# Queries and keys of two attentions as seven block products with their parts in DRAM, gates among the attention's steps, softmax scaling on ScalarE

## The chip, the cores and the metric

The kernel runs on one core of one Trainium2 chip. A core has a matrix engine (TensorE, PE in the profile), a vector engine (VectorE, DVE), a scalar engine (ScalarE, ACT), a general one (GpSimd, POOL) and a sequencer that issues DMAs (SyncE, SP). Each engine works through its own list of instructions in order, and waits there until what the instruction needs is ready. The metric is the device time of one execution in microseconds (us), the median of several runs.

## The reference

Two layers work on 512 rows of 1024 float32 numbers. A layer projects its input x with one wide matrix, runs three mixers on the pieces, gates and sums them, and ends in a feed-forward block (SwiGLU), with a layer norm after each half. Cut to what matters here:

```python
h = jnp.einsum('bsd,de->bse', x, w_in[l])
rq, rk, rv, rg, cq, ck, cv, dq, dk, dv, gates = jnp.split(h, splits, axis=-1)
o_a = _retention(rq, rk, rv, rg, ret_norm_g[l])
o_b = _chunk_attention(cq, ck, cv, ca_rel_bias[l])          # 8 heads of 64
o_c = _diff_attention(dq, dk, dv, lam, lambda_init, ...)    # 4 pairs of heads of 64
g = jax.nn.sigmoid(gates + b_merge[l]).reshape(B, S, N_BRANCHES, D)
merged = g[:, :, 0] * (o_a @ w_a) + g[:, :, 1] * (o_b @ w_b) + g[:, :, 2] * (o_c @ w_c)
x = _layer_norm(ALPHA * x + merged @ w_out[l], ...)
u_gate, u_up = jnp.split(x @ w_ffn_in[l], 2, axis=-1)
x = _layer_norm(ALPHA * x + (silu(u_gate) * u_up) @ w_ffn_out[l], ...)
```

The four projections cq, ck, dq and dk are 512 columns wide each, cv and dv 512, rv and rg 1024, and the gates 3072. In chunk attention a softmax weight is exp(score) divided by its row's sum. In differential attention the queries and keys are turned by rotary tables first, and each head pair combines two softmaxes, p0 - lam p1, before it is multiplied with the values.

## The kernel before

**Numbers.** Every float32 operand of a matrix product is carried as a pair, a high part rounded by a copy on ScalarE (`part_hi`) and a low part, the rest, subtracted on VectorE (`part_lo`). `mm3` (L122 to L125) makes one product of pairs in three matmuls: high by high, high by low, low by high.

**Weights.** `Wt` (L129) is a weight tile of 256 columns and eight blocks of 128 rows. It is loaded into one of four stage buffers `st` and split into `wh` (ScalarE, L155) and `wl` (VectorE, L156), of which there are three each; the split is done in two halves. `run_items` keeps three weight tiles fetched ahead, so an item's split is in the engines' lists some two items before its matmuls.

**Seven products.** `u_two` (L716) computes two 512-wide projections that share the input as block products by seven instead of eight (the form of Winograd): the input and the weights are cut into 2 x 2 blocks, `Quarters.turned` makes sums of input blocks (`s12`, `s43`), `Adds` (L214) makes sums of weight blocks, partly by loads that accumulate on the way (issued by POOL), and `Staged` (L255) casts and subtracts a 2048-wide block (L261, L262). Before the change three such problems run per layer: the two value projections of chunk and differential attention (`w`), and two for retention's values and gates (`p`, `q`). Each of the seven is a list item of its own, called m1, m2, y, x, g, h, v. `product` puts rows of x on the output's partitions; `product_T`, which the feed-forward part uses, puts output columns there, as two 256-wide matmul groups.

**Queries and keys.** Those of chunk and differential attention are projected directly: `u_cqk(p)` (L869) and `u_dqk(h)` (L937) each project 128 columns of queries and 128 of keys for one pair of heads, 48 matmuls of 512 columns, and hand the result to `QK` (L362), whose `set_q` and `set_k` write the high and low parts into the layout that the scores need: a head's 64 rows in one half of the partitions and another part in the other half. `u_dqk` applies the rotary tables first.

**Attention in steps.** Chunk attention's head h has three steps: `s_c1` (scores, `softmax_num` at L392, then the reciprocal and the scaling by it at L899 on VectorE), `s_c2` (`transpose_triangle` at L407: ten transposes on TensorE, parts on the other engines), `s_c3` (product with the values). In differential attention a head pair has `s_d0` twice (scores of its two heads), `s_d1` (the combination on VectorE, L970), `s_d2` (transposes), `s_d3` (product with the values, copy, squares, a power on POOL, output scaling at L1014) and `s_d4` (transposes of the output and its parts `och`, `ocl`).

**Order.** The items of a layer stand in one list (L1094 to L1112). Beside each item stand groups of steps: `between()` is called after each half of an item and runs the next group, so the steps of the attention lie between halves of projections. The projections are the fill: matmuls that TensorE can do while the other engines work on a softmax. `c(i)` and `d(i)` give the two groups for the i-th place of chunk and differential attention. The build then keeps this order on each engine, with small shifts by its own scheduler. Gates (`u_gate`, 48 matmuls of 512 columns, a tanh) are computed ahead of the branch products (`u_branch`); those named in `EARLY` (six of the twelve) are stored to DRAM and read back, since the 61 slots of the pool `gp` don't hold all. After the third branch's four products comes the output projection with `mg`, the merged result's pairs.

## Time and profile before

| | |
|---|---|
| median of 3 runs | 1900.33 us (1900.01 to 1900.47) |
| profiled execution | 1898.38 us |
| its span in the profile | 1896.5 us |
| mean granted TensorE clock | 0.999 |
| instructions | 26422 |

The span goes from the first to the last instruction of the program; the execution's own time has 1.9 us more around it. All durations quoted from here on are from this one execution.

In the views, PE is the matmul part of TensorE and PEld its weight loads, which run beside the matmuls. A row of the groups gives line, engine, operation, output and inputs with their shapes, how many, then busy time and the mean of one, then idle time just before them and what ended it. A row of the windows gives for each engine its busy time and, in brackets, its number of instructions, then the granted clock of TensorE, the share of the DMA engines and GB/s. A row of a timeline gives start and duration in us; in square brackets stands how long the engine had been idle, and whose result ended that.

### The profile page before, as it was taken

Reading aid. Unit: us, or ns where it says so; the run is one execution under the profiler, and the core shown is the slowest. Engines: PE = TensorE matmul, PEld = TensorE weight load, DVE = VectorE, ACT = ScalarE, POOL = GpSimd, SP = SyncE. Lnnn points to the kernel's source line nnn. Section 1 sums busy time; section 2 is a strip of 40 time slices with the busy share of each in tenths; the row PEclk is TensorE's granted clock in tenths of the full one; section 3 lists DMA queues with packets and bytes.
Section 4 is the critical chain, followed back from the end, with each engine's and each line's share of the span. In section 5 each row is a group of like instructions: output and inputs, shape, how many; then the busy total and the mean of one; then the engine's idle time right before and its main releaser. Section 6 shows DMA issues by size and latency. Waiting matters only on the chain. (4 is left out here: it accounts for less than half of the span.)

```text
span 1896.5 us, 26422 instructions
## 1 busy us (share of the span) xinstructions
PE 1873.9 (99%) x10354; PEld 1630.4 (86%) x10354; DVE 1358.4 (72%) x2065; ACT 957.4 (50%) x1547; POOL 105.5 (6%) x117
## 2 busy tenths in 40 slices
PE   9999999999999999999999999999999999999998
PEld 7788888888888999988898888888888889999886
DVE  5877766667766877787587777566776678877866
ACT  4644555567644444444255546455765344444431
POOL 0000000000001000010000010000000010000100
PEclk9999999999999999999999999999999999999999
DMA  8685443332156387885546835433322654869851
GB/s 264 193 255 141 142 142 127 109 117 87 56 169 187 105 231 177 240 209 151 156 167 195 241 110 166 159 112 97 122 71 80 199 129 145 211 157 266 206 149 45
DMA packets 221745, 297.84 MB, mean 157 GB/s; under 512 B 9534, under 2 KB 116148, under 8 KB 221620
## 3 DMA queue, kind: packets, MB, share of 16 engines
q1 hardware_dynamic: 198388, 250.01, 39.9%
q0 software_dynamic: 23232, 46.14, 14.0%
q8 instruction: 81, 1.33, 0.3%
q14 instruction: 44, 0.36, 0.1%
HBM read 273.00 MB, written 23.12 MB: 156 GB/s over the span
## 5 line engine op out<-in xcount | busy, mean ns | idle before, releaser
L123 PE MATMUL pt<-xTh,wh 128*128 128x512 f32 (+1 forms) x1456 | 506.9, 349 | 1.3 <-ACT wh L261 1.3
L124 PE MATMUL pt<-xTl,wh 128*128 128x512 f32 (+1 forms) x1456 | 502.5, 345 | 2.1 <-DVE xTl L113 1.9
L125 PE MATMUL pt<-xTh,wl 128*128 128x512 f32 (+1 forms) x1456 | 502.1, 345 | 0.0
L262 DVE TENSOR_TENSOR wl<-st,wh 128x2048 fp32r<-128x2048 f32 x126 | 288.1, 2289 | 135.0 <-ACT wh L261 134.7
L261 ACT CAST wh<-st 128x2048 fp32r<-128x2048 f32 x126 | 240.0, 1910 | 227.4 <-PE pt L124 129.1
L124 PEld LDWEIGHTS pt<-xTl,wh 128*128 128x128 f32 x1456 | 276.1, 190 | 34.5 <-DVE xTl L113 2.3
L123 PEld LDWEIGHTS pt<-xTh,wh 128*128 128x128 f32 x1456 | 275.7, 190 | 34.8 <-ACT wh L261 1.7
L125 PEld LDWEIGHTS pt<-xTh,wl 128*128 128x128 f32 x1456 | 275.7, 189 | 34.0
L155 ACT CAST wh<-st 128x1024 fp32r<-128x1024 f32 (+1 forms) x204 | 188.1, 948 | 195.6 <-issue 71.1
L156 DVE TENSOR_TENSOR wl<-st,wh 128x1024 fp32r<-128x1024 f32 (+1 forms) x204 | 219.0, 1095 | 90.6 <-ACT wh L155 84.2
L123 PE MATMUL pf<-wh,hqh 128*128 128x512 f32 x224 | 87.5, 391 | 0.5 <-DVE z L1272 0.5
L124 PE MATMUL pf<-wl,hqh 128*128 128x512 f32 x224 | 87.2, 389 | 0.0
L125 PE MATMUL pf<-wh,hql 128*128 128x512 f32 x224 | 87.1, 390 | 0.0
L123 PE MATMUL pt<-s43h,wh 128*128 128x256 f32 x256 | 72.7, 284 | 2.6 <-ACT wh L261 2.6
L352 ACT COPY sw<-pt 32x512 f32<-32x512 f32 (+1 forms) x96 | 55.6, 579 | 34.8 <-PE pt L125 33.6
L123 PE MATMUL pt<-s12h,wh 128*128 128x256 f32 x256 | 72.4, 283 | 0.0
L124 PE MATMUL pt<-s12l,wh 128*128 128x256 f32 x256 | 72.4, 283 | 0.0
L125 PE MATMUL pt<-s12h,wl 128*128 128x256 f32 x256 | 72.4, 283 | 0.0
L124 PE MATMUL pt<-s43l,wh 128*128 128x256 f32 x256 | 72.4, 283 | 0.0
L125 PE MATMUL pt<-s43h,wl 128*128 128x256 f32 x256 | 72.4, 283 | 0.0
L123 PE MATMUL pf<-wh,xTh 128*128 128x512 f32 x144 | 56.3, 391 | 0.0
L125 PE MATMUL pf<-wh,xTl 128*128 128x512 f32 x144 | 56.2, 391 | 0.0
(284 smaller groups left out, 3834.6 us busy)
## 6 DMA issues: line engine op xcount, KB each, us to landing
st<-in_w_in SPq DMA_DIRECT2D x60, 1024.0 KB
st<-in_w_ffn_in SPq DMA_DIRECT2D x40, 1024.0 KB
st<-in_w_ffn_out SPq DMA_DIRECT2D x24, 1024.0 KB
st<-in_w_in SPq DMA_DIRECT2D x32, 512.0 KB
st<-in_w_ffn_in POOLq DMA_DIRECT2D x16, 1024.0 KB, 10.4
st<-in_w_ffn_out POOLq DMA_DIRECT2D x16, 1024.0 KB, 9.8
st<-in_w_in POOLq DMA_DIRECT2D x12, 1024.0 KB, 11.2
th<-th SPq DMA_DIRECT2D x48, 256.0 KB
```

What stands on the lines that cost most here:

```text
L123: nc.tensor.matmul(ps, lh, rh, start=start, stop=False, skip_group_check=more)
L124: nc.tensor.matmul(ps, lh, rl, start=False, stop=False, skip_group_check=more)
L125: nc.tensor.matmul(ps, ll, rh, start=False, stop=stop, skip_group_check=more)
L155: return [nc.scalar.copy(self.hi[:, a:b], self.st[:, a:b]), nc.vector.tensor_sub(self.lo[:, a:b], self.st[:, a:b], f(self.hi[:, a:b]))]
L156: nc.vector.tensor_sub(self.lo[:, a:b], self.st[:, a:b], f(self.hi[:, a:b]))]
L261: nc.scalar.copy(self.hi, st)
L262: nc.vector.tensor_sub(self.lo, st, f(self.hi))
L352: nc.scalar.copy(sw[half * b:half * b + half], ps[half * o:half * o + half])
```

## The change

- **Queries and keys.** `u_cqk` and `u_dqk` go. The chunk attention's two projections become one problem of seven products (`cc`), the differential attention's another (`dd`), both by `u_two` with `product_T`. Each assembled result (128 columns of the output by two times 256 rows) goes through `qk_away`: rotary where it belongs, high and low part on whole 128 x 512 tiles, and a store of each to DRAM. Before a head pair's scores, `qk_back` makes a `QK` and `fetch` reads its parts back in ten DMAs of 64 x 512. The zeros in `kl` that POOL writes stay. The rotary tables are loaded in halves (`rot_tables`), and the mask of differential attention has a step of its own (`mask`).
- **Gates.** The gate items stand among the attention's steps, where the direct projections stood; all but the last of them go through DRAM. Gate (0, 3) stands inside `dd`.
- **Two steps in a place.** c(5) with c(6) share one item, and d(6) with d(7).
- **Last branch.** Three of its four products become one item, `u_branch_by_row(2, 3, 2)`: six results in six PSUM banks, with the row blocks outside, and the last pair's transposes, value product and output transposes (`s_d4(2)`, `s_d2(3)`, `s_d3(3)`, `s_d4(3)`) between the row blocks. `branch_done` is the end of a branch product, unchanged and put into a function.
- **Weights** are split whole instead of in halves.
- **Scaling.** The chunk attention's division by the softmax sum goes from VectorE to ScalarE.

Over the program TensorE's list has 768 matmuls of 512 columns fewer and 1344 of 256 columns more; SP's has 746 DMAs instead of 482.

```diff
-EARLY = [(0, 0), (0, 1), (0, 2), (0, 3), (2, 0), (2, 1)]
+EARLY = [(br, i) for br in range(3) for i in range(4)][:-1]
...
             self.load(0, nk)
-            h = max(nk // 2, 1)
-            for a in range(0, nk, h):
-                self.split(a, min(a + h, nk))
+            self.split(0, nk)
...
-        def set_q(self, src, scale):
...
-        def set_k(self, src):
...
+        def fetch(self, away, c):
+
+            (qh, ql), (kh, kl) = away["q"], away["k"]
+            for j, own, oth in ((0, A, B), (1, B, A)):
+                for to, rows, src in ((self.q[j], own, qh), (self.q[j], oth, ql), (self.k[j], own, kh),
+                                      (self.k[j], oth, kh), (self.kl[j], own, kl)):
+                    nc.sync.dma_start(f(to[rows]), src[own, c])
...
-        def u_two(left, right, left_done, right_done):
+        def u_two(left, right, left_done, right_done, prod=product):
...
-                        use(j, functools.partial(product, xq, name, j, wt))
+                        use(j, functools.partial(prod, xq, name, j, wt))
...
-        def u_cqk(p):
...
+        def qk_away(away, name, scale, rot=None):
+
+
+            away[name] = [dram.tile([P, 2048], F32, name=f"{name}{part}{l}_{'cd'[rot is not None]}") for part in "hl"]
+
+            def done(i, src):
+                half, b = divmod(i, 2)
+                if rot is not None:
+                    src = rotary(src, rot["cd"][half], rot["sd"][half], 32)
+                hi, lo = g(F32R, "qkh"), g(F32R, "qkl")
+                part_hi(hi, src, scale)
+                part_lo(lo, src, hi, scale)
+                for t, to in zip((hi, lo), away[name]):
+                    to = to.rearrange("p (q c) -> p q c", c=512)[:, 2 * b:2 * b + 2, 256 * half:256 * half + 256]
+                    nc.sync.dma_start(to, f(t).rearrange("p (q c) -> p q c", c=256))
+            return done
+
+        def qk_back(qk, away, p):
+            def fn():
+                qk[p] = QK()
+                qk[p].fetch(away, slice(512 * p, 512 * p + 512))
+            return fn
...
-                    nc.vector.tensor_scalar_mul(e, e, r[:, nt:nt + 1])
+                    nc.scalar.activation(e, e, AF.Identity, scale=r[:, nt:nt + 1])
...
-        def u_dqk(h):
...
+        def rot_tables():
...
+        def mask():
...
+        def u_branch_by_row(br, n, m):
...
+            def fn(*wts):
+                act = (oa, ob, oc)[br]
+                jobs = [(wts[i], P * j, bank("pt")) for i in range(n) for j in range(2)]
+                th_ = [gate_of(br, d) for d in range(2 * n)]
+
+                def rows(k0, k1, jobs):
+                    for k in range(k0, k1):
+                        for wt, c0, ps in jobs:
+                            mm3(ps, wt.hi[:, k, c0:c0 + P], wt.lo[:, k, c0:c0 + P], act[k].hi, act[k].lo,
+                                k == 0, k == nk - 1)
+
+                for k in range(nk - 1):
+                    rows(k, k + 1, jobs[:2 * m])
+                    between()
+                rows(0, nk - 1, jobs[2 * m:])
+                between()
+                rows(nk - 1, nk, jobs)
+                for d, (t, job) in enumerate(zip(th_, jobs)):
+                    branch_done(br, d, t, job[2])
+            return [([w[:, 256 * i:256 * i + 256]], nk) for i in range(n)], fn
...
+        caw, daw = {}, {}
         w, p, q = u_two(CV, DV, v_away(cv, 64), v_away(dv, 128, -1.0)), u_rvg(0), u_rvg(1)
+        cc = u_two(CQ, CK, qk_away(caw, "q", CA_DH ** -0.5), qk_away(caw, "k", None), product_T)
+        dd = u_two(DQ, DK, qk_away(daw, "q", DA_DH ** -0.5, tabs), qk_away(daw, "k", None, tabs), product_T)
+        cb, db = functools.partial(qk_back, cqk, caw), functools.partial(qk_back, dqk, daw)
         for (specs, fn), *groups in [
...
-            (u_gate(2, 0), [s_r2(2)], [s_r2(3), s_r3(2)]), (u_cqk(1), [s_r3(3)] + c(0)[0], c(0)[1]),
-            (u_branch(0, 0), c(1)[0] + [v_back(cv)], c(1)[1]), (u_branch(0, 1), *c(2)), (u_cqk(2), *c(3)),
-            (u_branch(0, 2), *c(4)), (u_cqk(3), *c(5)), (u_branch(0, 3), *c(6)), (u_gate(2, 1), *c(7)),
-            (u_dqk(0), *c(8)), (u_gate(1, 0), [v_back(dv)], [s_c3(7)] + d(0)[1]), (u_branch(1, 0), *d(1)), (u_dqk(1),),
-            (u_gate(1, 1), *d(2)), (u_branch(1, 1), *d(3)), (u_dqk(2),),
-            (u_gate(1, 2), *d(4)), (u_branch(1, 2), *d(5)), (u_dqk(3),),
-            (u_gate(1, 3), *d(6)), (u_branch(1, 3), *d(7)), (u_gate(2, 2), [s_d4(2)], [s_d2(3)]),
-            (u_gate(2, 3), [s_d3(3)], [s_d4(3)]),
-            (u_branch(2, 0),), (u_branch(2, 1),), (u_branch(2, 2),), (u_branch(2, 3),),
...
+            (w["m1"],), (w["m2"], [lam]), (w["y"],), (w["x"],), (w["g"], [], [p["a"]]), (w["h"],), (w["v"], [s_dh(0)], [p["c"]]),
+            (p["m1"], [], [s_r1(0)]), (p["m2"], [s_dh(1)]), (p["y"], [], [s_r1(1)]), (p["x"],), (p["g"], [], [cc["a"]]),
+            (p["h"],), (p["v"], [], [cc["c"]]),
+            (cc["m1"], [], [s_r2(0)]), (cc["m2"],), (cc["y"], [s_r2(1)], [s_r3(0)]), (cc["x"], [], [s_r3(1)]),
+            (cc["g"], [], [dd["a"]]), (cc["h"], [rot_tables]), (cc["v"], [], [dd["c"]]),
+            (dd["m1"],), (dd["m2"],), (u_gate(0, 3),), (dd["y"],), (dd["x"],), (dd["g"], [], [q["a"]]), (dd["h"],),
+            (dd["v"], [], [q["c"]]),
+            (u_rqk(rq, RQ, 1),), (q["m1"], [s_dh(2)]), (u_rqk(rk, RK, 1),), (q["m2"], [], [s_r1(2)]), (q["y"], [s_dh(3)]),
+            (q["x"], [], [s_r1(3)]), (q["g"],), (q["h"], [], [cb(0)]), (q["v"],),
+            (u_gate(1, 0), [s_r2(2)], [s_r2(3), s_r3(2)]), (u_gate(1, 1), [s_r3(3)] + c(0)[0], c(0)[1]),
+            (u_branch(0, 0), [cb(1)] + c(1)[0] + [v_back(cv)], c(1)[1]), (u_branch(0, 1), *c(2)),
+            (u_branch(0, 2), [cb(2)] + c(3)[0], c(3)[1]), (u_branch(0, 3), *c(4)),
+            (u_gate(1, 2), [cb(3)] + c(5)[0] + c(5)[1], c(6)[0] + c(6)[1]), (u_gate(1, 3), *c(7)),
+            (u_gate(2, 0), [db(0), mask] + c(8)[0], c(8)[1] + [v_back(dv)]), (u_gate(2, 1), [], [s_c3(7)] + d(0)[1]),
+            (u_branch(1, 0), [db(1)] + d(1)[0], d(1)[1]), (u_branch(1, 1), *d(2)), (u_gate(2, 2), [db(2)] + d(3)[0], d(3)[1]),
+            (u_branch(1, 2), *d(4)), (u_branch(1, 3), [db(3)] + d(5)[0], d(5)[1]),
+            (u_gate(2, 3), d(6)[0] + d(6)[1], d(7)[0] + d(7)[1]),
+            (u_branch_by_row(2, 3, 2), [s_d4(2)], [s_d2(3)], [s_d3(3)], [s_d4(3)]), (u_branch(2, 3),),
```

Of the item list the first half of the removed lines and the unchanged ones are cut. How the lists of the engines move is shown at three places; a row has line, operation, output and inputs by the program's names, the shape, and how many follow each other.

The first place is TensorE's list at the first pair of differential attention in the first layer, at the transposes of the combined softmax `dE`. `xT` is the layer's input, `ob` the output of chunk attention, `wh` and `wl` the weights' parts. Before:

```order
L124 MATMUL pt<-xTl,wh 128x512
L125 MATMUL pt<-xTh,wl 128x512
L417 MATMUL ptr<-ident,dE 128x128 x10
L123 MATMUL pt<-xTh,wh 128x512
L124 MATMUL pt<-xTl,wh 128x512
```

and after:

```order
L124 MATMUL pt<-obl,wh 128x512
L125 MATMUL pt<-obh,wl 128x512
L412 MATMUL ptr<-ident,dE 128x128 x10
L123 MATMUL pt<-obh,wh 128x512
L124 MATMUL pt<-obl,wh 128x512
```

Before, 72 matmuls of 512 columns stand between the second scores of the pair and these transposes, projections and a gate; after, twelve, half of a branch product.

The second place is ScalarE's list at the second pair's second scores. L404 before and L399 after are the exponentials with their sums; L155 and L153 are casts of weights, L1044 a gate's tanh; the numbers tell buffers apart. Before:

```order
L1006 ACTIVATE junk_3907,ss_3905<-do_3906 128x128 x2
L155 CAST wh_3995<-st_3994 128x512 x2
L404 ACTIVATE dE_3961,sums_3964<-dE_3961,mx_3965 128x512
L404 ACTIVATE dE_3962,sums_3964<-dE_3962,mx_3965 128x384
L404 ACTIVATE dE_3963,sums_3964<-dE_3963,mx_3965 128x256
L404 ACTIVATE dE_3962,sums_3964<-dE_3962,mx_3965 128x128
L352 COPY sw_4035<-pt_4010 32x512 x4
```

and after:

```order
L1015 ACTIVATE junk_4690,ss_4688<-do_4689 128x128 x4
L153 CAST wh_4792<-st_4791 128x2048
L1044 ACTIVATE th_4754<-pt_4729,hb_370 128x512
L399 ACTIVATE dE_4758,sums_4761<-dE_4758,mx_4762 128x512
L399 ACTIVATE dE_4759,sums_4761<-dE_4759,mx_4762 128x384
L399 ACTIVATE dE_4760,sums_4761<-dE_4760,mx_4762 128x256
L399 ACTIVATE dE_4759,sums_4761<-dE_4759,mx_4762 128x128
L109 ACTIVATE och_4819<-pdt_4814,colv_368 128x512
```

Before, two quarter-size casts stand ahead of the exponentials; after, a whole cast (into a `wh` that an earlier item holds) and the tanh of the gate that is being computed.

The third place is VectorE's list at the end of the third branch in the first layer. L1065, L1069 and L115 are the gate's product, the sum over branches and the low part of the merged result `mgl`; L156 before and L154 after subtract the weights' low parts. Before:

```order
L156 TENSOR_TENSOR wl<-st,wh 128x512
L1065 SCALAR_TENSOR_TENSOR th<-th,pt 128x512
L1069 TENSOR_TENSOR th<-th 128x512
L115 SCALAR_TENSOR_TENSOR mgl<-th,mgh 128x512
L156 TENSOR_TENSOR wl<-st,wh 128x512 x2
L1065 SCALAR_TENSOR_TENSOR th<-th,pt 128x512
L1069 TENSOR_TENSOR th<-th 128x512
L115 SCALAR_TENSOR_TENSOR mgl<-th,mgh 128x512
L156 TENSOR_TENSOR wl<-st,wh 128x1024 x2
L1065 SCALAR_TENSOR_TENSOR th<-th,pt 128x512 x2
L1069 TENSOR_TENSOR th<-th 128x512 x2
L1065 SCALAR_TENSOR_TENSOR th<-th,pt 128x512
```

and after:

```order
L1065 SCALAR_TENSOR_TENSOR th<-th,pt 128x512 x2
L115 SCALAR_TENSOR_TENSOR mgl<-th,mgh 128x512
L1069 TENSOR_TENSOR th<-th 128x512 x2
L1065 SCALAR_TENSOR_TENSOR th<-th,pt 128x512
L115 SCALAR_TENSOR_TENSOR mgl<-th,mgh 128x512
L1069 TENSOR_TENSOR th<-th 128x512
L115 SCALAR_TENSOR_TENSOR mgl<-th,mgh 128x512
L1065 SCALAR_TENSOR_TENSOR th<-th,pt 128x512
L115 SCALAR_TENSOR_TENSOR mgl<-th,mgh 128x512
L1069 TENSOR_TENSOR th<-th 128x512
L115 SCALAR_TENSOR_TENSOR mgl<-th,mgh 128x512
L154 TENSOR_TENSOR wl<-st,wh 128x1024
```

Before, the low parts of weights alternate with one or two results' operations; after, seventeen full-width operations (thirteen of these rows' and four of the same lines just ahead of them) stand in a row ahead of the 1024-wide `wl`, which belongs to the last branch product.

61 lines of the change are left out of this document (21 added, 40 removed).

## The prediction

> **What bounds the kernel now.** First the page's head, the busy shares and the slices.
>
> ```profile
> span 1896.5 us, 26422 instructions
> PE 1873.9 (99%) x10354; PEld 1630.4 (86%) x10354; DVE 1358.4 (72%) x2065; ACT 957.4 (50%) x1547; POOL 105.5 (6%) x117
> PE   9999999999999999999999999999999999999998
> ```
>
> TensorE is busy in 1873.9 of 1896.5 us, in every slice. So time falls only with its own work, and any wait given to it is added in full. Next, its groups with shapes kept apart, and windows that hold one shape alone.
>
> ```profile
> L123 PE MATMUL pt<-xTh,wh 128*128 128x512 f32 x848 | 334.6, 395 | 0.0
> L123 PE MATMUL pt<-s43h,wh 128*128 128x256 f32 x256 | 72.7, 284 | 2.6 <-ACT wh L261 2.6
> ```
>
> ```profile
> core 0: us, PE busy (x) PEld busy (x) DVE busy (x) ACT busy (x) POOL busy (x), PEclk, DMA share, GB/s
> 29.00:61.70 32.70, 32.70 (x145) 27.09 (x145) 23.17 (x34) 18.08 (x25) 2.96 (x3) 1.00 1.02 296
> 613.00:652.00 39.00, 39.00 (x328) 39.00 (x327) 35.37 (x54) 20.05 (x30) 0.66 (x1) 1.00 0.14 48
> 399.00:476.00 77.00, 77.00 (x388) 65.54 (x387) 56.90 (x124) 52.18 (x118) 5.22 (x8) 1.00 0.28 90
> ```
>
> A matmul's own 395 or 284 ns overlap with the next; its price is the pitch: 32.7/145 = 0.2255 us for 512 columns and 39.0/328 = 0.119 us for 256, more than half, so narrow products give a part back. The third window is differential attention today: TensorE never waits while VectorE is busy 56.9 of 77 us, because full-width projections stand between the attention's steps.
>
> **The change part by part. The matmuls.** Per layer, four 512-wide projections are 384 matmuls of 512 columns. Two problems of seven products are 2 x 7 x 48 = 672 of 256. Both layers: -768 x 0.2255 = -173.2, +1344 x 0.119 = +159.8 us, together **-13.4 us**. Every other matmul stays.
>
> **The waits in differential attention.** Between the first scores and the last output of a layer stand today, as fill, three query/key items and five gates of 48 full-width matmuls each (10.8 us) and four branch-1 items of 24 (5.4); afterwards two gates, the four of branch 1 and the by-row item. The second scores of a head pair are followed by the pair's combination, and its transposes stood 16 us of fill later; now a half branch item or a half gate is there. How long the chain from scores to transposes takes is in the timelines of today's first pair, PE, DVE and ACT in turn.
>
> ```profile
> 406.18 0.39 PE L387 MATMUL psc<-ks,qs 128*128 128x512 f32 x1
> 407.39 0.44 PE L123 MATMUL pt<-xTh,wh 128*128 128x512 f32 x1
> ```
>
> ```profile
> 406.99 1.29 DVE L1069 TENSOR_TENSOR th<-th 128x512 f32<-128x512 f32 x2
> 408.19 0.68 DVE L402 CUSTOM_DVE_ANT_0 dE<-psc,mask 128x512 f32<-128x512 f32 x1
> 411.30 0.18 DVE L964 RECIPROCAL rec<-sums 128x4 f32<-128x4 f32 x1 [0.18 <-ACT dE L404]
> 411.98 1.94 DVE L970 SCALAR_TENSOR_TENSOR dE<-dE,rec 128x128 f32<-128x128 f32 x4
> 438.91 0.16 DVE L1010 SCALAR_TENSOR_TENSOR ss<-ss,sums 128x4 f32<-128x4 f32 x1 [0.76 <-ACT junk L1006]
> 440.26 1.31 DVE L1014 TENSOR_SCALAR do<-do,rsr 128x128 f32<-128x128 f32 x4 [1.19 <-POOL rsr L1011]
> ```
>
> ```profile
> 408.98 0.72 ACT L404 ACTIVATE dE<-dE,mx 128x512 f32<-128x512 f32 x1 [1.33 <-DVE mx L402]
> 411.08 0.19 ACT L404 ACTIVATION_READ_ACCUMULATOR dE<-dE,mx 128x1 f32 x1
> ```
>
> Columns: start, duration, line, operands, idle before. Scores take 1.2 us (406.18 to 407.39). From VectorE's first reduction, 408.19, the exponentials end 3.1 us later (411.27) and the combination 5.7 us later (411.98 + 1.94). A full-width VectorE operation has a pitch of 0.60 us (two from 406.99 to 408.19). Zero below is the start of a pair's second scores; ten transposes need 1.0 us.
>
> *Pair 0.* TensorE reaches the transposes after 1.2 + 12 x 0.2255 = 3.9 us. VectorE's order has a half split and branch operations first (reductions from 0.9) and one more add behind the reciprocal: 0.9 + 5.7 + 0.6 = 7.2; the last four transposes end at 7.7 instead of 4.9: **2.8**.
>
> ```profile
> L261 ACT CAST wh<-st 128x2048 fp32r<-128x2048 f32 x126 | 240.0, 1910 | 227.4 <-PE pt L124 129.1
> L262 DVE TENSOR_TENSOR wl<-st,wh 128x2048 fp32r<-128x2048 f32 x126 | 288.1, 2289 | 135.0 <-ACT wh L261 134.7
> L1035 ACT ACTIVATE th<-pt,hb 128x512 f32<-128x512 f32 x8 | 5.5, 684 | 3.5 <-PE pt L125 3.4
> L156 DVE TENSOR_TENSOR wl<-st,wh 128x1024 fp32r<-128x1024 f32 x26 | 31.3, 1222 | 5.8 <-ACT wh L155 2.9 <-PE ptr L417 2.6
> ```
>
> *Pair 1.* ScalarE's order has the cast of the next gate's weights ahead of the exponentials, and it waits for a buffer that the present gate gives back at zero: 1.91 + 0.68 for the tanh puts them at 2.6, their end at 4.9. Behind it VectorE does the reciprocal's group (0.7), a branch operation, a low part and an add (1.8), the combination (1.94): 9.3, transposes to 9.7 instead of 1.2 + 2.7 + 0.4 + 1.0 = 5.3: **4.4**. *Pair 2* has, by VectorE's order, a half split (1.22), pair 1's output scaling and two branch operations (1.2) among its four reductions. The scaling waits for POOL (ss at 438.91 to do at 440.26: 1.35, then 1.31), so the last reduction ends at 7.4, exponential and reciprocal's group at 8.1, the combination at 10.0 and the transposes at 10.3. TensorE has 1.2 + 5.4 + 0.4 + 1.0 + 0.4 = 8.4 without a wait: **2.0** at least. *Pair 3*: pair 2's output is scaled at 6.0, its transposes are reached at 3.9 (2.0); pair 3's own combination costs 0.3 more; its output runs through copies, squares, POOL and scaling for 5 us beside 18 matmuls (4.1 us), 0.9, and ScalarE's half of that output is waited for by the next matmul, 0.9: **4.1**.
>
> *The end of the by-row item.* Six results end within 3 us and each needs three full-width VectorE operations. The split of the last item's weights (wl, 1.22) stands behind 17 of them: 17 x 0.60 + 1.22 = 11.4 us, 12.0 with the casts it alternates with. TensorE can do 20 matmuls meanwhile (4.5 us): **7.5**. Before, each pair of results has 5.4 us of matmuls beside it.
>
> Per layer 2.8 + 4.4 + 2.0 + 4.1 + 7.5 = 20.8, twice **41.6 us**. Bounds: 0, as in the window 399 to 476, and about 30 per layer if each chain also queues behind ScalarE. I take the chains, since their rows are those of the same instructions.
>
> **The clock.** The end of the program shows what a long rest does.
>
> ```profile
> 1886.00:1890.00 4.00, 1.44 (x7) 0.86 (x5) 3.93 (x7) 0.00 (x0) 0.92 (x1) 1.00 0.31 120
> 1891.50:1896.50 5.00, 0.00 (x0) 0.00 (x0) 1.45 (x3) 0.00 (x0) 0.00 (x0) 0.50 0.29 107
> ```
>
> ```profile
> 83.30 0.39 PE L125 MATMUL pf<-wh,s12l 128*128 128x512 f32 x1
> 86.72 0.50 PE L123 MATMUL pf<-wh,s43h 128*128 128x512 f32 x1 [3.03 <-ACT tu L731]
> 87.06 0.40 PE L124 MATMUL pf<-wl,s43h 128*128 128x512 f32 x1
> ```
>
> The granted clock is 0.50 some 4 us after the last matmul, while after 3.03 idle us it hardly shows (87.06 - 86.72 = 0.34). So the 7.5 us wait should dip, and the others perhaps not. No row shows the return to full rate; between 0 and the 4 us that the fall takes I take 3 us at half rate, 1.5 lost, twice **3.0 us** (bounds 0 and 4 x 2). The Trainium skill's "TensorE: Matmul & The Clock Gate", Part 1, says that an idle window of about 3.4 us halves the clock and that as much busy time restores it. By it the 4.4 us wait dips too, four dips of 1.7 = 6.8, and the sum ends 3.8 us later; both rows agree with its limit, and no run here shows the return.
>
> **Transfers.** Accumulating loads have their own queue.
>
> ```profile
> q1 hardware_dynamic: 198388, 250.01, 39.9%
> q0 software_dynamic: 23232, 46.14, 14.0%
> ```
>
> ```profile
> 62.00:115.00 53.00, 49.97 (x221) 41.07 (x220) 37.25 (x47) 27.50 (x37) 2.56 (x2) 1.00 0.72 221
> 1000.00:1060.00 60.00, 60.00 (x266) 49.66 (x265) 43.20 (x58) 31.92 (x44) 2.56 (x2) 1.00 0.76 227
> ```
>
> 250.01 MB in 39.9% of 1896.5 us is 330 GB/s, 46.14 in 14.0% is 174. A problem loads 5.24 MB plainly and 2.10 accumulating (15.9 + 12.1 us); with 4.19 MB of parts written (12.7) it needs 40.7 us, beside 336 x 0.119 = 40.0 us of matmuls. Value, chunk and differential problems are like this, and the gate that stands in the first one today moves out. Of today's two value problems (0.72 and 0.76 share) one waits 3.03 us and one does not, so I add one such wait, **3.0 us** (bounds 0 and six, 18). A store that waits on SP for its low part holds the weight loads queued behind it, and TensorE needs those two items later.
>
> **Costed at nothing.**
>
> ```profile
> L899 DVE TENSOR_SCALAR cE<-cE,rec 128x512 f32<-128x512 f32 x8 | 3.9, 482 | 0.0
> ```
>
> The softmax scaling, four operations of at most 0.482 per head, leaves VectorE for ScalarE; an item's matmuls stand between it and the transposes (uncovered: 1.9 x 16 heads). Reading a pair back is 1.3 MB, 4 us at 330 GB/s, issued two items ahead (uncovered 4 x 16). Casts of whole 2048-wide weights instead of halves, rotary on assembled rows, extra adds: they lie beside 40 us per problem, in which VectorE has nine full-weight operations (20.6) and fourteen of 0.60 (8.4), 29 us; the differential problem's rotary adds 24 x 0.60 = 14.4 and its gate a split, 46 of 51 us. What doesn't fit would be a wait for weights of up to one cast, 1.91. POOL's clears are unchanged.
>
> **Sum.** -13.4 + 41.6 + 3.0 + 3.0 = +34.2 us: span 1930.7. The profiled execution's 1898.38 becomes 1932.6; the median of the runs, 1900.33, lies 1.95 above it: **1934.5 us**.
>
> **The rivals.** *Faster.* The fill suffices: for it, today's attention windows without any wait, and VectorE's average of 74%. It decides where the five waits of a layer fall below 6.7 us in sum; with none, 1900.3 - 13.4 = 1886.9. Against it: two of them (4.4, 7.5) hang on orders in which one instruction stands behind another. Chance 0.13. *Half the waits.* Pairs 0, 2 and 3 find VectorE free, only 4.4 and 7.5 stay: -13.4 + 23.8 = +10.4, 1910.7; chance 0.13. *Transfers bind.* Six waits of 3.0 instead of one: 1949.5; for it, 40.7 us of transfers in 40.0; against, 296 GB/s at a share of 1.02 in the window 29 to 61.7 with no wait; 0.12. *The clock dips at every wait over 4 us*, the 4.4 too: four dips of 1.7 instead of 3.0, 1938.3; 0.15, since 3.03 us left the rate full and about 4 us halved it, and 4.4 lies at the edge. The Trainium skill's page named above is for it. *That the seven products aren't made*: no, the order shows 1344 matmuls of 256 columns for 768 of 512.
>
> **How the numbers follow.** The forecast has 0.47. The range, 1906 to 1955, takes in half the waits and the transfers with some 5 us for the unknown costs at both ends; outside it are the faster case (0.13), 0.03 below 1906 and 0.04 above. 0.2% (3.8 us) is what a measurement of this kernel can tell from no change. Faster 0.13, same 0.03, slower 0.84.
>
> **What would show it.** Right: TensorE idle of 2 to 8 us at the transposes of dE (released by the combination line), and one of 7 us before the last item's pt matmuls, released by wl; the slices of TensorE below 9 near both attention ends; product groups of 2.9 us per 24. Wrong: no idle there, or one as long before the first product of a problem, released by a DMA.

## The result, and the profile after

The changed kernel takes 2025.46 us (median of 4 runs, 2020.88 to 2026.46), the kernel before 1900.20 in the same comparison: 1.0654 times as long, 95% interval 1.0636 to 1.0673. The direction was forecast; the size was not: 125 us were lost where 34 were expected, and the time lies 70 us above the range. The page's head of the profiled execution (2020.88 us), busy shares, TensorE's slices and its granted clock:

```profile
span 2019.1 us, 28019 instructions
PE 1912.4 (95%) x10930; PEld 1677.0 (83%) x10930; DVE 1366.3 (68%) x1916; ACT 972.6 (48%) x1486; POOL 112.0 (6%) x125
PE   9989989999899999999999899899998899999998
PEclk9989989999899999999999999898998999999999
```

The span is 122.6 us longer. Two lines carry this. TensorE rests 2019.1 - 1912.4 = 106.7 us instead of 22.6, **84.1 more**. And it is busy 38.5 us longer, though its list should have become 13.4 us shorter: its matmuls took **51.9 us more** than at the pitches of before. Five of the clock row's six dents stand in slices where PE has one too. The waits of TensorE, grouped by what released them (us in total, times, longest):

```profile
PE ptr L412 <- DVE dE L979: 18.0, 6, 4.8
PE pf L123 <- ACT tm L726: 16.1, 2, 8.1
PE pt L125 <- DVE wl L154: 13.4, 2, 6.7
PE pco L934 <- DVE cPl L113: 9.0, 4, 3.0
PE pf L123 <- ACT tu L726: 8.4, 4, 4.9
PE pt L123 <- ACT wh L153: 7.4, 3, 3.7
PE pco L934 <- DMA vhl<-v: 6.5, 6, 2.2
PE pf L123 <- DVE rtmp L782: 6.2, 3, 5.3
PE pt L123 <- ACT och L109: 1.6, 2, 0.8
```

By place: differential attention 18.0 + 13.4 + 1.6 = 33.0 us; the block products and the gate behind them 16.1 + 8.4 + 7.4 + 6.2 = 38.1; chunk attention 9.0 + 6.5 = 15.5. Only the first of these places had a large term in the prediction. (A wait is given here as the idle time that the views show; the expectations further down count it from the starts of the matmuls, which makes the same wait 0.1 to 0.2 us longer.)

The slower matmuls are for the most part a matter of the clock. In this windows view the columns are those of before; the first row is a wait of 8 us, the next two what follows, the last two the same behind the by-row item:

```profile
287.80:295.80 8.00, 0.00 (x0) 0.00 (x0) 7.16 (x10) 4.77 (x7) 0.00 (x0) 0.70 0.84 264
295.90:300.90 5.00, 5.00 (x12) 3.66 (x13) 4.00 (x7) 2.84 (x6) 0.00 (x0) 0.50 0.28 94
300.90:305.90 5.00, 5.00 (x27) 4.31 (x26) 3.73 (x7) 2.15 (x4) 0.00 (x0) 0.97 0.00 0
603.60:610.20 6.60, 0.03 (x1) 0.00 (x0) 6.60 (x12) 3.40 (x6) 0.00 (x0) 0.86 0.00 0
610.30:614.70 4.40, 4.39 (x10) 3.47 (x11) 4.40 (x3) 0.00 (x0) 0.00 (x0) 0.50 0.70 235
```

After a wait the granted clock is 0.50 for some 5 us, and 12 matmuls of 512 columns fill 5.0 us (0.417 each instead of 0.2255). TensorE counts as busy in them. The trace's record of the granted clock has 19 such stretches ahead of the program's end, each 3.4, 6.8 or 10.2 us long, 116 us together; the kernel before has none there. TensorE is busy in 89.7 of these 116 us, and half of that, some 45 us, is what the half rate costs (an estimate); the other 7 of the 51.9 us it does not explain.

What VectorE waited for, of DMAs, in the kernel before and then in the changed one:

```profile
DVE th L1065 <- DMA th<-th: 10.4, 8, 2.9
DVE tb L891 <- DMA tb<-nrel: 0.9, 1, 0.9
```

```profile
DVE th L1065 <- DMA th<-th: 25.4, 12, 6.0
DVE tb L901 <- DMA tb<-nrel: 22.4, 11, 5.9
DVE rtmp L782 <- DMA dh<-in_decay: 10.0, 3, 5.1
```

The gates read back, the bias tables and the decay tables are late now. On average the plain queue has room (it went from 39.9% to 45.1%). What holds a table back shows in the timeline of the changed kernel in chunk attention, SyncE's, VectorE's and ScalarE's rows in turn:

```profile
444.58 0.59 SPq L377 DMA_DIRECT2D kl<-kl_c  x1
445.27 0.53 SPq L892 DMA_DIRECT2D tb<-nrel  x1
449.30 0.11 DVE L901 MEMSET tb<- 64x64 f32 x1 [5.94 <-DMA tb<-nrel]
449.34 0.11 DVE L905 RECIPROCAL rec<-sums 128x4 f32<-128x4 f32 x1
449.37 0.65 DVE L113 TENSOR_TENSOR cPl<-ptr,cPh 128x512 fp32r<-128x512 f32 x1
449.48 1.92 ACT L909 ACTIVATE cE<-cE,rec 128x128 f32<-128x128 f32 x4 [4.21 <-DVE rec L905]
451.31 0.56 ACT L107 CAST cPh<-ptr 128x512 fp32r<-128x512 f32 x1
```

Ten reads of a pair's queries and keys are issued from 438.95 to 445.2, one behind the other; the next head's bias table comes after them and is there at 449.3. VectorE stands 5.94 us at the memset of that table. Behind it in its list are this head's reciprocal and a low part (`cPl`) for which TensorE waits; ScalarE stands at the scaling, which needs the reciprocal, and behind the scaling is the cast for TensorE's next wait. The DMA engines are half free in the four us before the table lands, but full at the other waits of chunk attention, those for its values `vhl` (share and GB/s stand at the end):

```profile
445.30:449.30 4.00, 1.80 (x8) 1.14 (x7) 0.00 (x0) 0.00 (x0) 0.00 (x0) 1.00 0.52 145
386.00:390.00 4.00, 1.89 (x9) 1.22 (x8) 1.62 (x3) 2.25 (x5) 0.00 (x0) 0.99 1.07 385
```

### The profile page after: what moved, and what is told of

It is laid out like the page before. It is cut to its first block, busy times and chain, and to the rows that moved or that the text cites. A ratio compares the mean times of both kernels' runs of the same rounds, so it can differ in the third digit from the quotient of the medians.

```text
span 2019.1 us, 28019 instructions
## 1 busy us (share of the span) xinstructions
PE 1912.4 (95%) x10930; PEld 1677.0 (83%) x10930; DVE 1366.3 (68%) x1916; ACT 972.6 (48%) x1486; POOL 112.0 (6%) x125
## 3 DMA queue, kind: packets, MB, share of 16 engines
q1 hardware_dynamic: 213364, 303.51, 45.1%
## 5 line engine op out<-in xcount | busy, mean ns | idle before, releaser
L123 PE MATMUL pt<-xTh,wh 128*128 128x256 f32 (+1 forms) x1392 | 461.2, 332 | 9.3 <-ACT wh L153 7.4
L124 PE MATMUL pt<-xTl,wh 128*128 128x256 f32 (+1 forms) x1392 | 458.4, 330 | 1.9 <-DVE xTl L113 1.6
L125 PE MATMUL pt<-xTh,wl 128*128 128x256 f32 (+1 forms) x1392 | 457.9, 329 | 0.0
L260 DVE TENSOR_TENSOR wl<-st,wh 128x2048 fp32r<-128x2048 f32 x154 | 352.3, 2290 | 132.3 <-ACT wh L259 131.0
L259 ACT CAST wh<-st 128x2048 fp32r<-128x2048 f32 x154 | 293.6, 1909 | 246.7 <-PE pt L124 139.4
L154 DVE TENSOR_TENSOR wl<-st,wh 128x2048 fp32r<-128x2048 f32 (+2 forms) x91 | 171.9, 1892 | 149.4 <-ACT wh L153 118.5
L153 ACT CAST wh<-st 128x2048 fp32r<-128x2048 f32 (+2 forms) x91 | 144.1, 1587 | 233.6 <-PE pt L124 99.3
L123 PEld LDWEIGHTS pt<-s43h,wh 128*128 128x128 f32 x384 | 73.6, 192 | 3.0 <-ACT wh L259 3.0
L123 PEld LDWEIGHTS pt<-s12h,wh 128*128 128x128 f32 x384 | 73.7, 192 | 0.1
L124 PEld LDWEIGHTS pt<-s12l,wh 128*128 128x128 f32 x384 | 73.7, 192 | 0.1
## 6 DMA issues: line engine op xcount, KB each, us to landing
st<-in_w_in POOLq DMA_DIRECT2D x20, 1024.0 KB, 11.6
```

Source lines behind the costliest of these rows:

```text
L123: nc.tensor.matmul(ps, lh, rh, start=start, stop=False, skip_group_check=more)
L124: nc.tensor.matmul(ps, lh, rl, start=False, stop=False, skip_group_check=more)
L125: nc.tensor.matmul(ps, ll, rh, start=False, stop=stop, skip_group_check=more)
L153: return [nc.scalar.copy(self.hi[:, a:b], self.st[:, a:b]), nc.vector.tensor_sub(self.lo[:, a:b], self.st[:, a:b], f(self.hi[:, a:b]))]
L154: nc.vector.tensor_sub(self.lo[:, a:b], self.st[:, a:b], f(self.hi[:, a:b]))]
L259: nc.scalar.copy(self.hi, st)
```

## The experiments

All ratios are to the kernel before on the same chip; "the changed kernel" stands for 1.0654 (1.0636 to 1.0673). A step of 0.001 is 1.9 us, and "us less" is worked out from the ratios. Busy and idle times are those of the one profiled execution of each kernel.

**The reads of queries and keys from another queue.**

```diff
-                    nc.sync.dma_start(f(to[rows]), src[own, c])
+                    nc.gpsimd.dma_start(f(to[rows]), src[own, c])
```

> The 160 reads of queries and keys are issued by GpSimd instead of SyncE; nothing else is changed. Theory (SyncE's queue): each of these small reads takes SyncE 0.55 to 0.6 us to issue, ten are 5.6 us, and the bias tables, the chunk values and the gates that stand behind them in its list land late; VectorE or TensorE wait for those. Then the waits of TensorE at 387 to 394 us (2.3 + 0.8 + 0.9) and at 447 to 453 (3.1 + 2.1) of the first layer go, and their like in the second, 18 us in all, with some 6 us of half-rate matmuls behind them: about 2000 us. Rival (transfers as such): the bytes and packets are the same, so the waits stay, and the time is within 5 us of the changed kernel's 2025. Second rival: GpSimd issues them no faster and behind its accumulating loads, so the reads themselves come late and the wait moves to the scores: within 10 us either way.

2018.89 us, 1.0636 (1.0612 to 1.0660): no difference from the changed kernel that is clear of the noise. The waits in chunk attention went, all but some 2 us a layer, but the first wait of differential attention grew from 4.8 to 11.4 us, and from 4.4 to 10.9 in the second layer. The waits of this kernel's TensorE and VectorE have these rows:

```profile
PE ptr L412 <- DVE dE L979: 29.7, 4, 11.4
DVE th L1065 <- DMA th<-th: 37.0, 15, 6.9
```

And VectorE's timeline, between the two scores of the first pair:

```profile
498.54 0.69 DVE L1065 SCALAR_TENSOR_TENSOR th<-th,pt 128x512 f32<-128x512 f32 x1 [6.95 <-DMA th<-th]
```

VectorE now stands at a gate read back. So the place in SyncE's list was the cause at the bias table of 449 us, where VectorE's wait fell from 5.94 to 1.33. (For bias tables in all it still waits 23.5 us, mostly where TensorE does not wait for it.) GpSimd also issues the reads earlier (the second pair's from 356.7 us instead of 374.5), so at the chunk values, where the DMA engines are full, place and transfers are not told apart. In differential attention the next late load of SyncE's list took the gain away.

**The reads half an item earlier** (`cb` and `db` moved behind the scores of the pair before).

> The changed kernel with each head pair's reads of queries and keys (all but the first pair of each attention) put half an item earlier in the list, behind the scores of the pair before, so that bias tables, chunk values and gate reads no longer stand behind ten of them. Still all on SyncE, the same bytes. Theory (place in SyncE's queue): the waits in chunk attention (9.2 and 8.9 us a layer) fall to 4 or less a layer, and the first wait in differential attention (4.9), of which VectorE's 1.6 us for a gate is a part, to about 3; with the half-rate stretches some 18 us less, a ratio to before of about 1.056. Rival (too many bytes or packets at these places): the waits stay, and the ratio is 1.062 or more.

2048.23 us, 1.0793 (1.0775 to 1.0811): 26 us worse. VectorE's waiting for gates rose to 43.9 us in 13 times; the first wait in differential attention became 8.0 us. The ratio is the rival's, 1.062 or more. That moving the ten reads forward put the gates behind them is a reading of the order in SyncE's list; no further run tells it from the rival's reason, too many bytes at these places.

**Bias tables two heads ahead, the second branch's gates an item earlier.**

> The changed kernel with chunk attention's bias tables loaded two heads ahead instead of one, and the gates of the second branch read back an item earlier; the reads of queries and keys stay where they are. Theory (VectorE stands in its list at a small load that lands late): of the waits in chunk attention those released by parts of transposed weights go (3.1 + 2.1 us a layer), those for chunk values stay (2.3 + 0.8 + 0.9); the first two waits in differential attention (4.9, 3.9) lose the 1.6 and 0.9 us in which VectorE waits for a gate. Some 7 us a layer with 2 us of dips: 15 to 20 us less, a ratio to before of 1.055 to 1.058. Rival (the queue as a whole is behind, so that what is put first makes another load late, as when the reads were put earlier): 1.062 or more.

2023.34 us, 1.0651 (1.0636 to 1.0667): no change. VectorE's waits for bias tables fell only to 17.7 us. The first differential wait was 5.5 us with the gate there in time, for the build had put operations on branch results ahead of the second reductions, as VectorE's timeline of this kernel shows:

```profile
512.28 0.69 DVE L1074 SCALAR_TENSOR_TENSOR th<-th,pt 128x512 f32<-128x512 f32 x1 [0.99 <-PE pt L125]
513.00 0.69 DVE L1078 TENSOR_TENSOR th<-th 128x512 f32<-128x512 f32 x1
513.61 0.68 DVE L397 CUSTOM_DVE_ANT_0 dE<-psc,mask 128x512 f32<-128x512 f32 x1
```

The rival held. Which load is late depended on the order; that some load is late at these places did not, in the orders tried here.

**The decay table two items earlier.**

```diff
-(w["g"], [], [p["a"]]), (w["h"],), (w["v"], [s_dh(0)], [p["c"]]),
+(w["g"], [s_dh(0)], [p["a"]]), (w["h"],), (w["v"], [], [p["c"]]),
```

> The first decay table of retention is loaded two items earlier (beside w's g instead of w's v). Theory: the 5.5 us wait of TensorE at 112 us of the first layer is VectorE's wait of 5.1 us for this load, which is issued behind six stores and lands 11 us later. It goes, with the half-rate stretch behind it (3.0 us): 8 us less; the next wait (3.1 us at 133) stays. Rival: VectorE has too much to do there, and the bank would come free late anyway: less than 3 us.

2014.72 us, 1.0613 (1.0594 to 1.0632), 8 us less. In the timeline of the changed kernel, SyncE's rows and then VectorE's, the table is issued behind six stores and VectorE waits 5.1 us for it:

```profile
99.02 6.17 SPq L847 DMA_DIRECT2D v<-vhl  x6
105.25 0.46 SPq L765 DMA_DIRECT2D dh<-in_decay  x1
116.67 0.69 DVE L782 TENSOR_TENSOR rtmp<-psr,dh 128x512 f32<-128x512 f32 x1 [5.10 <-DMA dh<-in_decay]
```

The 6.2 us of waits released by `rtmp` went, but those released by `tu`, one item later, rose from 8.4 to 12.2, and TensorE's rest as a whole fell by 1.2 us only (from 106.7 to 105.5); its busy time fell by 4.9. The 8 us are the theory's number, then, but only in part its mechanism: the next wait, which was to stay, grew.

**The last split ahead of the results** (the by-row item's six results are finished inside the next item).

```diff
...
                 act = (oa, ob, oc)[br]
+                while late:
+                    branch_done(*late.pop(0))
                 for j in range(2):
...
-                for d, (t, job) in enumerate(zip(th_, jobs)):
-                    branch_done(br, d, t, job[2])
+                late.extend((br, d, t, job[2]) for d, (t, job) in enumerate(zip(th_, jobs)))
```

> The six results of the by-row item are finished inside the last branch item, so that the split of the last item's weights stands ahead of all but two of their seventeen VectorE operations. Theory (as predicted: the low part of the last weights is late because it stands behind them): the wait of 6.9 us before the last branch product falls to 2 or less in each layer, with the half-rate stretch behind it (2.0 us): 10 to 14 us less in all. Rival: the splits of the output projection's weights now come ahead of the results, and the wait moves to the first output products, which need the merged result: less than 4 us.

2003.58 us, 1.0552 (1.0534 to 1.0571), 19 us less, more than the theory's 10 to 14. The 13.4 us of waits released by `wl` are gone, and no new row took their place; the other waits grew by some 4 us in all (TensorE's rest is 97.4 us instead of 106.7), and its busy time fell by 8.1. VectorE's timeline has the split behind two operations instead of seventeen:

```profile
602.70 1.28 DVE L1067 SCALAR_TENSOR_TENSOR th<-th,pt 128x512 f32<-128x512 f32 x2 [0.96 <-PE pt L125]
604.02 1.22 DVE L154 TENSOR_TENSOR wl<-st,wh 128x1024 fp32r<-128x1024 f32 x1
```

**Without rotary in the differential problem** (left out, so its queries and keys are not turned).

> The rotary step of the differential attention's queries and keys is left out (four copies on ScalarE, three operations on VectorE for each of 16 results). Theory (VectorE and ScalarE fall behind in that problem, and the copies and parts of retention's queries stand behind it in their lists): the waits at 287 us (8.2) and 320 us (3.8) of the first layer and their like in the second fall below 3 us in sum per layer, with their half-rate stretches (2.3 + 1.6): about 25 us less. Rival: these waits come from retention's own rotary and decay steps, which stand close together now: at most 5 us less.

1995.96 us, 1.0514 (1.0491 to 1.0536), 27 us less. The 16.1 us released by `tm` are gone, 7.4 became 4.4 at the gate, and the 6.2 released by `rtmp` became 2.8, while those released by `tu` rose from 8.4 to 11.1. The theory held: in the window 287.8 to 295.8 above VectorE is busy 7.16 of 8 us while TensorE rests; the parts and rotary of retention's queries stand in its list behind the end of the differential problem.

**Scaling back on VectorE.**

```diff
-                    nc.scalar.activation(e, e, AF.Identity, scale=r[:, nt:nt + 1])
+                    nc.vector.tensor_scalar_mul(e, e, r[:, nt:nt + 1])
```

> The changed kernel with the softmax scaling back on VectorE, nothing else. Theory: the scaling costs 1.9 us a head on either engine and in the same chain (reciprocal, scaling, transposes), and VectorE stands idle there, waiting for bias tables: within 4 us of the changed kernel's 2025. Rival: ScalarE is what holds the parts of the transposed weights back (its scaling stands ahead of their casts), and the waits of TensorE in chunk attention shrink by 1 us or more each: 8 us less or better.

2011.85 us, 1.0593 (1.0576 to 1.0611): 12 us less, the rival's size. TensorE's waits in chunk attention are these, instead of 9.0 and 6.5:

```profile
PE pco L934 <- DVE cPl L113: 6.8, 2, 3.5
PE pco L934 <- DMA vhl<-v: 3.9, 5, 1.0
PE pco L934 <- DVE wl L154: 1.6, 1, 1.6
```

That is 12.3 instead of 15.5 us, less than the rival's 1 us for each wait. Most of the gain is the clock's: the stretches at 0.50 in chunk attention are 6.8 us long together, where the changed kernel has 30.7. With the scaling on VectorE, ScalarE has nothing that waits for the late reciprocal, and its casts go on. VectorE's own waiting for bias tables rose to 34.2 us.

**Splits in halves again.**

> The changed kernel with weights split in two halves again, nothing else. Theory: whole splits cost at most one cast at each place where TensorE waits for a weight; of those the trace shows the start of the gate behind retention's last problem (3.8 us, released by the cast) and the last branch product (6.8, released by the low part): with halves each gets shorter by up to 1 us, so 0 to 6 us less. Rival: whole casts ahead of the exponentials are what makes the differential attention late; its waits (4.9 and 3.9 us) shrink by 1 us or more each: 8 us less or better.

2014.35 us, 1.0607 (1.0581 to 1.0634), 9 us less; the interval ends just below the changed kernel's. The waits that the theory named are shorter (the last branch product 4.9 us instead of 6.7, the gate 2.8 and 2.6 instead of 3.7 and 3.5), and so is the second wait of differential attention (3.0 and 2.8 instead of 3.7 and 3.6). But the first one there grew (5.3 and 5.2 instead of 4.8 and 4.4), and so did those behind the differential problem (9.1 each instead of 8.1). In sum TensorE rests as long as before (107.4 us, 106.7 in the changed kernel), and what fell is its busy time, by 7.6 us, with 16 stretches at half rate instead of 19. How much of this the halves make and how much the place of the waits stays open.

**TensorE kept busy in a wait** (28 spare matmuls ahead of the last branch product).

> The changed kernel with 28 spare matmuls of 512 columns (6.3 us at full rate) ahead of the last branch product, into the bank that this product then starts anew: TensorE is busy in the 6.8 us in which it waits for the low part of the weights. Theory (a rest costs its own length and then some 4 us at half rate): the wait for the low part ends at the same time, but the 12 matmuls behind it keep 0.2255 us each instead of about 0.43 (611 to 615 us of the first layer, 2.0 us lost): 3 to 4 us less in all. Rival: they are slow for another reason (their operands, transfers), and stay so: no change, or a few tenths more.

2019.49 us, 1.0634 (1.0619 to 1.0650). The time alone would not tell 4 us; the windows do. From 607 to 614.5 the spare matmuls run, and the product behind them:

```profile
607.00:614.50 7.50, 7.35 (x33) 5.76 (x31) 7.50 (x13) 4.77 (x7) 0.00 (x0) 1.00 0.00 0
614.90:619.30 4.40, 4.25 (x19) 3.52 (x20) 4.40 (x4) 0.00 (x0) 0.00 (x0) 1.00 0.62 224
```

19 matmuls in 4.25 us at a clock of 1.00, where the changed kernel ran 10 in 4.39 at 0.50, with the same weights and transfers. So the rest before them is what halves the rate.

**Half of the change**: only chunk attention's queries and keys as seven products; differential attention keeps its projections and its place.

> The kernel before with only chunk attention's queries and keys as seven products by way of DRAM, the differential attention with its direct projections and all its fill as before, the scaling on VectorE, weights split in halves, six gates through DRAM; four items less stand beside chunk attention, whose heads share three items in pairs or threes. Matmuls: 6.7 us less than before. Theory (lost fill, rotary in the problem and late small loads are separate causes, each at its own place): no wait in the differential attention nor behind the problems; in chunk attention the late loads (9 us a layer) stay and the crowded items add some 7: 1915 to 1940 us. Rival (the problems and their transfers as such slow everything): waits before retention's second problem and in the differential attention as in the changed kernel, above 1945.

1934.92 us, 1.0193 (1.0176 to 1.0209). As the theory had it, nothing waits in differential attention. TensorE rests 29.5 us more than in the kernel before. Some 24 of these lie in chunk attention, where the bias tables are late; some 6 lie in the block products, where the waits released by `tu` rise from 4.1 to 10.3. VectorE's and TensorE's rows in chunk attention:

```profile
DVE tb L922 <- DMA tb<-nrel: 43.7, 13, 6.4
PE pco L955 <- DVE cPl L113: 16.6, 9, 3.1
```

The changed kernel loses 88 us more. Between the two stand differential attention's problem and the gates in place of its projections, but also the by-row item, the scaling on ScalarE, whole splits and five more gates through DRAM, so the 88 us cannot be put down to any one of them.

**That half mended.** Bias tables two heads ahead; then the fill spread over chunk attention, with gate (0, 2) from the start of the layer; then that gate back and heads in pairs.

> The half change of the earlier run (chunk attention's queries and keys alone as seven products) with the bias tables loaded two heads ahead, nothing else. Theory: VectorE's 43.7 us of waiting for these tables falls below 15, and of TensorE's waits in chunk attention (13 and 11 us a layer) at most half is left: 10 to 15 us less with dips, a ratio of 1.011 to 1.014. Rival (the heads are too crowded, three items in pairs or threes): 1.017 or more.

> That kernel with the fill spread: gate (0,2) goes from the start of the layer to chunk attention, gate (0,3) into retention's first problem, the decay table earlier, so that no item holds three heads. Theory: chunk attention waits 3 us a layer or less, nothing else does beyond before: 1893 to 1905 us, a ratio of 0.997 to 1.003. Rival (fill taken from the start of the layer is missing there, or the heads in pairs still wait): 1.006 or more.

> The half change with the fill spread as before, but gate (0,2) back at the start of the layer; heads 2 and 3, 4 and 5, 6 and 7 of chunk attention share an item in pairs. Theory: the waits at the start of the layers (6.4 and 4.8 us, and 4.2 of dips) go, the heads in pairs add 2 us a layer at most: 1899 to 1906, a ratio of 1.000 to 1.004; the 6.7 us of saved matmuls are then just eaten by what is left. Rival (the pairs need the fill that goes): 1.008 or more.

1933.71 us, 1.0181 (1.0164 to 1.0198): no gain, the tables still cost VectorE 38.1 us. 1919.03 us, 1.0096 (1.0079 to 1.0113): the waits in chunk attention fell to 2.5 and 4.3 us in the two layers, but at the start of each layer 4.6 us of waits are new. 1917.78 us, 1.0109 (1.0093 to 1.0125), no better: those went, and chunk attention waits 9.1 and 9.4 us, most of it for VectorE's product with a gate. An earlier spread with the last branch by rows and gates mixed into the differential attention gave 1965.00:

> Chunk attention's queries and keys alone as seven products (6.7 us of matmuls less than before), with the gates spread for it: gate (0,3) in retention's first problem, gate (1,0) beside chunk attention, reads half an item earlier, the decay table earlier, the last branch by rows with its split first, scaling on VectorE, splits in halves. Direct projections still fill the differential attention. Theory: with fill at each place and small loads early, waits stay within 6 us of before's: 1893 to 1903. Rival (four items of fill are gone whatever their order): chunk attention still waits 5 us or more a layer, with dips: 1908 or more.

1.0355 (1.0339 to 1.0370). Its scores in differential attention wait for parts of queries and keys whose projection had ended just before (11.6 us, released by ScalarE). No version beat the kernel before.

**Mends together**: decay table, last split and scaling, with the reads earlier, and then with the small loads instead.

> The changed kernel with four single edits together: decay table earlier, last split first, softmax scaling on VectorE, reads earlier. Theory (separate causes): what they save adds up, less some 6 us where scaling and reads mend the same wait: 45 to 58 us less than the changed kernel, 1967 to 1980; left are the waits behind the differential problem (8.2 + 3.8 a layer) and those of the head pairs' chains. Rival (one backlog that comes up wherever it is let): what is mended at one place is lost at the next, and more than 1990 stays.

> The same with the decay table earlier, the last split first and the softmax scaling on VectorE. Theory (separate causes): the single savings in ratio, 0.0041 + 0.0102 + 0.0061 and 0.009 for this one, add up: 1.036, about 1966 us; left are the waits behind the differential problem and those of the head pairs' chains. Rival (what is mended comes up elsewhere): 1.050 or more.

2006.78 us, 1.0577 (1.0561 to 1.0592), and 1990.10 us, 1.0477 (1.0462 to 1.0493). The expected sums failed because the reads and the small loads failed. With what these did by themselves (+0.0139 and -0.0003) the single steps, -0.0204 for the other three, add to 1.0589 and 1.0447: within 0.003 of both, which is less than the intervals of four or five such numbers leave open. This sum was made afterwards. So the decay table, the last split and the scaling are separate places, whose gains add up. The loads are another matter: where one was put first, another was late.

## Why the prediction was wrong, step by step

The measured sum is -13.4 + 84.1 + 51.9 = 122.6 us of span: the matmuls' saving as forecast, waits of 84.1 where the text had 41.6 and 3.0, and slower matmuls of 51.9 where it had 3.0. Of the waits, some 50 lie at places that the text costed at nothing.

- **Matmuls, -13.4.** This held. A window of the changed kernel with chunk attention's products alone, 240 matmuls in 28.5 us, has the pitch of before, 0.119:

```profile
186.50:215.00 28.50, 28.50 (x240) 28.50 (x239) 16.26 (x16) 14.67 (x18) 1.33 (x1) 1.00 0.79 224
```

- **Waits in differential attention, +41.6.** The mechanism was right, the size near: 33.0. The end of the by-row item was put at 7.5 and was 6.7, and the experiment that moved the split took just this away. Pair 1 was put at 4.4 and was 3.7 and 3.6. Pair 0, put at 2.8, was 4.8 and 4.4, part of it a gate that VectorE waits 1.58 us for in the first layer; pairs 2 and 3, put at 2.0 (10.3 less 8.4 is 1.9) and 4.1, were 0.8 and 0.8. That the sum comes near is in part luck: pair 0 is too small, and pairs 2 and 3 are too large.
- **Clock, +3.0.** The first step that failed. I let only waits over some 4 us dip, from one wait of 3.03 us that did not. The changed kernel has 19 dips, among them some after waits of 2.9 and even of 2.1 us, and the half change has a wait of 3.2 without any; the last section shows what decides. All slower matmuls together are 51.9 us, and a us of waiting cost 1.6 us in all (84.1 + 51.9 over 84.1). The rule of the Trainium skill, "TensorE: Matmul & The Clock Gate", Part 1, that an idle window of 3.4 us halves the rate, gave the kind of loss and its length (the record's stretches are multiples of 3.4 us), but a window that was idle for less than half of its length halved it here too (1.57 of 3.41 us).
- **Rotary, gates and extra adds, costed at nothing.** The second. "46 of 51 us" for VectorE was an average over the problem, with the cover it named; what it left out is what stands behind: retention's rotary and parts in the same list. Without the rotary 16.1 us of waits go, 3.0 of the 7.4 at the gate, and 27 us of time. The longest of these waits, 8.1 us, stands ahead of a product of retention's second problem, but a copy on ScalarE ends it and not a DMA, as the text had it for such a place.
- **Reading a pair back, costed at nothing, and transfers, +3.0.** The third. I priced bytes (1.3 MB at 330 GB/s) and looked for a wait before a product; what counted was the place in SyncE's list, where ten reads take 6.2 us to issue and small loads for VectorE and the chunk values stand behind them: 15.5 us of waits in chunk attention, of which 6.5, for the values, fall where the DMA engines are full. At the decay table, which stands behind six stores, it is 6.2 us. In the rows above TensorE waits for a DMA only for chunk attention's values, so the wait of 3.0 for a problem's transfers was not seen as such.
- **Scaling, costed at nothing** since matmuls stand between it and the transposes. It was not the 1.9 us a head but the wait for the reciprocal that it carries to ScalarE: 12 us of time, 3.2 of them less waiting in chunk attention and the most of the rest shorter stretches at half rate there.
- **Range.** The text gave the uncovered cost of these items (1.9 x 16 and 4 x 16 us), and the range then took 5 us for all of them. With their own bounds it would have reached beyond 2025.

## What to carry to other kernels

Where the bound engine is busy 99% of the time, its fill is what pays for every chain elsewhere, and work that is taken off it must be set against what its waits then cost, the halved rate behind each included. An edit costed at nothing keeps its uncovered price in the range. And a queue that issues DMAs is an engine with a list: ten small reads cost little to move and 6 us to issue, and whatever an in-order engine needs next stands behind them.

## What was not expected of the hardware

After waits of 2.1 to 8.1 us the granted clock was 0.50 for stretches of 3.4, 6.8 or 10.2 us, while a wait of 3.03 us in the kernel before and one of 3.24 in the half change left it at 1.00. The traces show what decides. In each run the clock changes only at instants that lie whole multiples of 3.413 us apart (in the changed kernel all 19 stretches keep to this within 3 ns). Here the span is cut into slices at these instants: the 3.03 us wait of the kernel before, then the 3.24 us wait of the half change, then the changed kernel at a wait of 2.12 us and at two short ones of 0.6 and 1.3 us near 718 us. Behind the time stands TensorE's busy time; the granted clock is the third number from the end.

```profile
81.87:85.28 3.41, 1.82 (x9) 1.16 (x7) 0.63 (x3) 1.08 (x2) 0.00 (x0) 1.00 1.02 348
85.28:88.70 3.42, 1.98 (x9) 1.64 (x10) 2.36 (x2) 3.42 (x4) 0.00 (x0) 1.00 0.69 244
81.27:84.69 3.42, 1.88 (x9) 1.23 (x7) 0.52 (x2) 0.82 (x1) 0.00 (x0) 1.00 1.02 330
84.69:88.10 3.41, 1.71 (x7) 1.43 (x8) 2.36 (x2) 3.41 (x5) 0.00 (x0) 1.00 0.64 244
386.53:389.94 3.41, 1.29 (x6) 0.74 (x5) 1.62 (x3) 1.72 (x4) 0.00 (x0) 1.00 1.07 387
389.94:393.35 3.41, 2.59 (x7) 1.12 (x5) 0.00 (x0) 0.00 (x0) 0.00 (x0) 0.50 1.05 384
717.62:721.03 3.41, 1.84 (x11) 1.45 (x12) 3.15 (x2) 2.50 (x3) 0.00 (x0) 1.00 1.10 271
721.03:724.45 3.42, 3.42 (x18) 3.42 (x18) 2.54 (x3) 0.00 (x0) 0.00 (x0) 0.50 1.06 404
```

The two longer waits lie across an instant and share their rest between two slices; the clock stays. The 2.12 us lie in one slice, and the next has 0.50. The two short waits near 718 us lie for the most part in one slice too, with 1.57 us of rest, and 0.50 follows; the same two in the kernel before fall into two slices, 1.27 and 0.66, and the clock stays at 1.00. In the changed kernel all 19 stretches follow a slice in which TensorE rested 1.57 us or more of 3.41, and none follows one with 1.43 or less. Over all 18 kernels of this case, their first and last 20 us left out, 2.0 us of rest or more in a slice at full rate were always followed by half rate and 1.3 or less never; between them both occur. At half rate, 0.6 us of rest or more kept the next slice at 0.50, and 0.4 or less brought 1.00 back. So it is the rest in a slice that counts, not the length of one wait. Two kernels with the same rest can then differ by some us of matmul time by where their waits fall, and the single savings above hold a share of this.
